# A decoder trunk in float32: the weight ring in pairs, and the 7-product sets at other places

## The chip, the cores and the metric

One core of one Trainium2 chip. The time is device microseconds of one execution; a kernel's time is the median of its runs. In the profile, PE is TensorE's matmul, PEld its weight load, DVE VectorE, ACT ScalarE, POOL GpSimd, SP SyncE, whose queue issues most DMAs.

## The reference

Four layers, sequence 256, width 1024, all float32. Each layer is a half-step SwiGLU feed-forward block (FFN, inner width 2816), a token mixer with memory cross-attention, and a second FFN; the mixers are a gating MLP (layers 0 and 3), dilated window attention (layer 1) and forgetting attention (layer 2).

```
def swiglu_ffn(x, w_gate_up, w_down):
    gate, up = jnp.split(x @ w_gate_up, 2, axis=-1)
    return (jax.nn.silu(gate) * up) @ w_down
...
for i in range(DEPTH):
    kind, j = i % 3, i // 3
    g = norm_g[i]
    x = x + 0.5 * rms_norm(swiglu_ffn(rms_norm(x, g[0]), ffn_w_gate_up[i, 0], ffn_w_down[i, 0]), g[1])
    h = rms_norm(x, g[2])
    ...  # y = mixer a, b or c of h and the normalized memory
    x = x + rms_norm(y, g[3])
    x = x + 0.5 * rms_norm(swiglu_ffn(rms_norm(x, g[4]), ffn_w_gate_up[i, 1], ffn_w_down[i, 1]), g[5])
```

## The kernel before

**Products in three parts.** Every float32 operand is split into a rounded part `hi` and a rest `lo` (`split`: ACT copies to `hi`, DVE subtracts to get `lo`), and a product is hi·hi + hi·lo + lo·hi, accumulated in PSUM.

**The weight ring.** The host packs all weights in the order of use into units of 128 x 1024. `plan()` lists the units: g and u (a quarter of the rows of a gate or up set of 512 columns), e (the same for a set of half width, gate and up in one), D (one block of 128 rows of the down weight), R, C, K, V and O in the mixers, and S (below). `load_next` fetches a unit into one of 5 `raw` tiles over SP's queue; `split_next` makes `hi` and `lo` of it in a ring of 10 tiles each, and asks for the next raw unit. `take` hands a unit to PE's code; `slot(free)`, called once for each unit that PE has read, counts the units released, issues one quadrant load if one is due, takes one background step (`bg`), and calls `pump`, which splits up to two more units as long as the ring has room: about 8 units ahead of PE.

**The FFN** (`ffn`). The 22 blocks of 128 inner columns are cut into six sets (`WIDTH`, four blocks each, one set with two). The first set runs in two halves of the rows and holds its 8 g/u units for both. Two of the others run plainly (`half`), the one of half width too, and three as *7-product sets* (`SEVEN`, `seven`): a 2x2 block product in seven products instead of eight (Strassen-Winograd). For these the four weight quadrants b11, b12, b21, b22 (`quad`, 1 MB each) are loaded whole, in 8 loads in the order b11, b21, b12, b22; a DMA from POOL's queue adds b22 to b12 (`gather`, L271); operation 2 adds b12 to b11 on DVE (L285) and b11 to b21 by another such DMA; operation 4 subtracts b22 from b11 (L288). The seven operands are split into two S units each (`S` with operation and half), and PE multiplies them with sums of the input's quadrants (`left`), 6 products of 512 columns a unit, where other units have 12. Between operations, copies (`snap`, L632) and sums (L644, L655, L661, L666, L667) move between PSUM and SBUF: an operation that adds on to a bank must wait for the copy or the reading of that bank.

The products with the down weight (D units, `fill`) are put between the sets by the table `FILL`; the last 8 run at the end, over the first half of the rows and then over the second, while the norm's steps (`ln_stages`: ACT's squares, DVE's L378, L382, L389, two small operations on POOL at L351 and L352) and the transposes of the result (L403, split into `xth`/`xtl`) run beside them. `new_quad` begins the loads of a set's quadrants: for the first 7-product set ahead of the first set, for the others at the start of the set ahead of them. The tiles of the quadrants are shared with the mixers' `mgh`, `mgl` and with the norm's `rows`, so a load also waits for their last readers.

**Order.** The code is written in program order; a scheduler in the tile layer may move instructions of an engine where their operands come later, and each tile's next user waits for its last reader.

Of the kernel before, what the change touches and what calls it, by code (L numbers as in the profile page):

```python
# [10 lines left out]
F32 = mybir.dt.float32  # L11
# [7 lines left out]
P = 128  # L19
# [11 lines left out]
LN_EPS = 1e-5  # L31
BIG = 1e30
RING = 10
RAW = 5
HELD = 8
GRP = 4

# [168 lines left out]
class Trunk:  # L206
    def __init__(self, ctx, tc, io):
        self.ctx, self.tc, self.nc, self.io = ctx, tc, tc.nc, io
        pool = lambda name, bufs=1, **kw: ctx.enter_context(tc.tile_pool(name=name, bufs=bufs, **kw))
        self.const = pool("const")  # L210
        self.wp = pool("wp")
        self.main = pool("main")
        self.small = pool("small", 4)
        self.ps = pool("ps", space=bass.MemoryType.PSUM)
        self.dram = pool("dram", space=bass.MemoryType.DRAM)
        self.plan = plan()
        self.offs = {}
# [5 lines left out]
        self.raw_order = [key for key in self.plan if key[0] != "S"]  # L223
        self.loaded = self.split_n = self.taken = self.released = 0
# [5 lines left out]
        self.quad_loads = deque()  # L230

    def rot(self, *shape):
        t = self.ps.tile([P, 512], F32, tag="rot", name="rot", bufs=4)
# [10 lines left out]
    def load_next(self):  # L244
        if self.loaded == len(self.raw_order):
            return
        key = self.raw_order[self.loaded]
        a, b = unit_shape(key)
        t = self.wp.tile([P, 1024], F32, tag="raw", name="raw", bufs=RAW)
        self.fetch(t[:, :a * b], key)  # L250
        self.raws.append((t, a * b))
        self.loaded += 1

    def new_quad(self, fp, l, f, s):
        self.quad = [None] * 4
        self.quad_pool = fp
        self.quad_set = (l, f, s)
        self.quad_loads = deque(quads(l, f, s))

# [13 lines left out]
    def quads_for(self, key):  # L273
        if self.quad is None or self.quad_set != key[1:4]:
            return None
        return max(0, len(self.quad_loads) - (QUADS - ((2 * key[4] if key[4] < 2 else 6) + key[5] + 1)))
# [5 lines left out]
    def operand(self, op, h):  # L282
        b11, b12, b21, b22 = (t if t is None else t[:, h, :] for t in self.quad)
        if op == 2:
            self.nc.vector.tensor_tensor(out=b11, in0=b11, in1=b12, op=ALU.add)  # L285
            self.gather(b21, b11)
        elif op == 4:
            self.nc.vector.tensor_tensor(out=b11, in0=b11, in1=b22, op=ALU.subtract)  # L288
        return (b11, b21, b11, b12, b11, b21, b22)[op]

    def split_next(self):
        key = self.plan[self.split_n]
        hi = self.wp.tile([P, 1024], F32R, tag="hi", name="hi", bufs=RING)
        lo = self.wp.tile([P, 1024], F32R, tag="lo", name="lo", bufs=RING)
        if key[0] == "S":
            for _ in range(self.quads_for(key)):
                self.load_quad()
            self.split(hi, lo, self.operand(*key[4:]))
        else:
            t, n = self.raws.popleft()  # L300
            self.split(hi[:, :n], lo[:, :n], t[:, :n])
            self.load_next()
        self.ready.append((hi, lo))
        self.split_n += 1

    def pump(self, lag=1, most=2):
# [230 lines left out]
    def ffn(self, l, f, post_next, pre_next, last=False):  # L537
        nc, tc = self.nc, self.tc
        with tc.tile_pool(name=f"ffn{l}{f}", bufs=1, reuse_waits="tile") as fp:
# [15 lines left out]

            def turn_set(s, t):
                if t == 0:
                    if WIDTH[s] == 2:
                        hs[s] = tuple(fp.tile([P, 2, SEQ], F32R, tag=n, name=n) for n in ("eh", "el"))
                    else:  # L560
                        hs[s] = tuple(fp.tile([P, 4, SEQ], F32R, tag=n, name=n, bufs=2) for n in ("hh", "hl"))
                n = WIDTH[s]
                ps = self.rot()
                for k in range(n):
                    nc.tensor.transpose(ps[:, k * P:(k + 1) * P], T[s][t][:, k * P:(k + 1) * P], self.ident)  # L565
                self.split(*(h[:, :n, t * P:(t + 1) * P] for h in hs[s]),
                           ps[:, :n * P].rearrange("p (k t) -> p k t", k=n))
# [3 lines left out]
            def first_set():  # L571
                T[0] = [tile_T(), tile_T()]
                held = [self.take("g", l, f, 0, i) for i in range(4)]
                for t in range(2):
                    g = self.rot()
                    for i in range(4):
                        pair(held[i], g, i, t)
                        self.slot(t)
                    silu(T[0][t], g)
                    u = self.rot()  # L580
                    if t == 0:
                        held.extend(self.take("u", l, f, 0, i) for i in range(4))
# [5 lines left out]
                    nc.vector.tensor_tensor(out=T[0][t], in0=T[0][t], in1=u, op=ALU.mult)  # L588
# [189 lines left out]

    def mem_kv(self, l):
        nc = self.nc  # L780
        km = self.mp.tile([P, 2, SEQ], F32, name="km")
        vm = self.mp.tile([P, 2, SEQ], F32, name="vm")
# [58 lines left out]
        return got[0]  # L841

    def q_mem(self, l, c0, xt):
        qm = self.mp.tile([P, 2, SEQ], F32, name="qm")
# [503 lines left out]
```

## Time and profile before

| | before |
|---|---|
| median of 3 runs | 1889.15 us (1886.43 to 1889.77) |
| the profiled execution | 1888.2 us, span 1886.4 us |
| mean granted clock | 0.996 |
| HBM read | 359.95 MB |

The span is the time from the first to the last instruction of the profiled execution; the execution's own time has 1.8 us more around it. A group's line gives the busy time, the mean of one in ns, and the idle time ahead of it with what ended it. A row of waits gives the total in us, how many, and the longest. A matmul's busy time includes its passage through the array, in which the next one may already run.

### The profile page before, as it was taken

The page shows a single profiled execution, that of the slowest core. Times are in us where ns is not written, and L with a number is a line of the kernel's source. Part 1 is how long each engine was busy: PE and PEld are TensorE (multiplying, and loading weights), DVE is VectorE, ACT ScalarE, POOL GpSimd, SP SyncE. Part 2 cuts the span into 40 slices and gives each one's busy share as a digit, 9 for nine tenths or more (in the row PEclk, how much of TensorE's full clock was granted, in tenths as well). Part 3 has the DMA queues.
Part 4 walks back from the last instruction along what each step waited for, and adds up shares of the span by engine and source line. Part 5 has one row for each costly group of instructions (what it writes and reads, how often), then busy time and mean ns, then how long its engine had stood idle before and what let it go on. Part 6 is the DMA issues. An engine that isn't in the chain of part 4 may idle for free.

```text
span 1886.4 us, 25346 instructions
## 1 busy us (share of the span) xinstructions
PE 1842.0 (98%) x9310; PEld 1535.2 (81%) x9310; DVE 1537.1 (81%) x1868; ACT 1132.7 (60%) x1541; POOL 150.2 (8%) x211
## 2 busy tenths in 40 slices
PE   7999999999999999999999999999999999999998
PEld 5788887878788797778878889877788888987886
DVE  6888878987988768888789876879887988879884
ACT  5666656656665655656666666556665666656652
POOL 0000201000100100100010000010001000201000
PEclk9999999999999999999999999999999999999999
DMA  8886748776786662677668667358775786738862
GB/s 295 257 265 225 224 136 264 227 243 223 226 261 194 235 220 101 201 242 247 215 210 263 211 218 257 105 190 256 247 245 169 245 264 204 247 125 273 256 192 78
DMA packets 117692, 413.01 MB, mean 219 GB/s; under 512 B 13620, under 2 KB 18112, under 8 KB 117440
## 3 DMA queue, kind: packets, MB, share of 16 engines
q1 hardware_dynamic: 103568, 359.47, 54.2%
q0 software_dynamic: 14000, 51.92, 13.8%
q8 instruction: 73, 1.20, 0.3%
q14 instruction: 51, 0.42, 0.1%
HBM read 359.95 MB, written 1.06 MB: 191 GB/s over the span
## 4 chain that ended last, share of the span: by engine, by line
PE 41%; DVE 7%; DMA 3%; issue 2%; ACT 1%; POOL 1%; DVEq 0%; ACTq 0%; POOLq 0%
PE acc L696 12%; PE rot L624 9%; PE rot L337 5%; PE rot L339 5%; PE rot L338 5%; DVE lo L313 5%; PE acc L960 2%; DMA quad<-quad 2%; DMA quad<-in_w 1%; PE rot L565 1%; PE acc L880 1%; DVE quad L288 1%; PE rot L894 1%; PE rot L862 1%; ACT hi L312 0%
## 5 line engine op out<-in xcount | busy, mean ns | idle before, releaser
L313 DVE TENSOR_TENSOR lo<-raw,hi 128x1024 fp32r<-128x1024 f32 (+2 forms) x451 | 536.3, 1217 | 77.6 <-ACT hi L312 74.7
L312 ACT ACTIVATE hi<-raw 128x1024 fp32r<-128x1024 f32 (+2 forms) x451 | 463.2, 1051 | 198.3 <-DMA raw<-in_w 96.7
L312 ACT ACTIVATE hi<-quad 128x1024 fp32r<-128x1024 f32 x336 | 343.6, 1053 | 227.5 <-DVE quad L285 131.8
L313 DVE TENSOR_TENSOR lo<-quad,hi 128x1024 fp32r<-128x1024 f32 x336 | 397.5, 1219 | 20.7 <-ACT hi L312 19.9
L339 PE MATMUL rot<-hi,xtl 128*128 128x512 f32 (+3 forms) x816 | 312.8, 384 | 3.9 <-DVE xtl L313 3.9
L337 PE MATMUL rot<-hi,xth 128*128 128x512 f32 (+3 forms) x816 | 315.0, 386 | 0.4 <-ACT hi L312 0.4
L338 PE MATMUL rot<-lo,xth 128*128 128x512 f32 (+3 forms) x816 | 312.0, 382 | 0.3 <-DVE lo L313 0.3
L624 PE MATMUL rot<-hi,sums 128*128 128x512 f32 x768 | 255.1, 398 | 16.2 <-ACT snap L632 8.0
L696 PE MATMUL acc<-hi,hh 128*128 128x512 f32 x640 | 199.4, 391 | 0.0
L696 PE MATMUL acc<-lo,hh 128*128 128x512 f32 x640 | 198.9, 390 | 0.0
L696 PE MATMUL acc<-hi,hl 128*128 128x512 f32 x640 | 197.9, 390 | 0.0
L624 PEld LDWEIGHTS rot<-hi,sums 128*128 128x128 f32 x768 | 145.8, 190 | 52.9 <-ACT snap L632 12.3
L339 PEld LDWEIGHTS rot<-hi,xtl 128*128 128x128 f32 x816 | 153.7, 188 | 37.0 <-DVE xtl L313 8.3
L337 PEld LDWEIGHTS rot<-hi,xth 128*128 128x128 f32 x816 | 153.8, 189 | 29.2 <-ACT hi L312 1.0
L338 PEld LDWEIGHTS rot<-lo,xth 128*128 128x128 f32 x816 | 153.8, 188 | 29.2 <-DVE lo L313 0.5
L624 PE MATMUL rot<-lo,sums 128*128 128x512 f32 x384 | 151.2, 394 | 2.1 <-DVE lo L313 2.1
L271 POOL DMA_DIRECT2D quad<-quad x96 | 83.7, 897 | 837.6 <-DMA quad<-in_w 394.5
L696 PEld LDWEIGHTS acc<-hi,hl 128*128 128x128 f32 x640 | 119.6, 188 | 26.9 <-DVE hl L313 2.2
L696 PEld LDWEIGHTS acc<-lo,hh 128*128 128x128 f32 x640 | 119.9, 188 | 24.7
L696 PEld LDWEIGHTS acc<-hi,hh 128*128 128x128 f32 x640 | 119.7, 188 | 24.5
L624 PE MATMUL rot<-hi,xtl 128*128 128x512 f32 x288 | 112.1, 389 | 0.0
L624 PE MATMUL rot<-hi,xth 128*128 128x512 f32 x288 | 112.0, 389 | 0.0
(214 smaller groups left out, 2571.3 us busy)
## 6 DMA issues: line engine op xcount, KB each, us to landing
raw<-in_w SPq DMA_DIRECT2D x440, 512.0 KB, 4.8
quad<-in_w SPq DMA_DIRECT2D x192, 512.0 KB, 5.1
quad<-quad POOLq DMA_DIRECT2D x96, 512.0 KB, 4.7
gpre<-in_norm_g SPq DMA_DIRECT2D x8, 512.0 KB, 6.3
gpost<-in_norm_g SPq DMA_DIRECT2D x8, 512.0 KB, 3.4
memraw<-in_mem_t SPq DMA_DIRECT2D x32, 128.0 KB, 3.6
g<-in_norm_g SPq DMA_DIRECT2D x8, 512.0 KB, 6.7
raw<-in_w SPq DMA_DIRECT2D x8, 384.0 KB, 4.1
```

Source lines behind the costliest of these rows:

```text
L271: self.nc.gpsimd.dma_start(out=x, in_=y, accum_op=ALU.add)
L288: self.nc.vector.tensor_tensor(out=b11, in0=b11, in1=b22, op=ALU.subtract)
L312: self.nc.scalar.activation(out=hi, in_=src, func=AF.Copy)
L313: self.nc.vector.tensor_tensor(out=lo, in0=src, in1=hi.bitcast(F32), op=ALU.subtract)
L337: mm(out, a[0], b[0], start=start, stop=False)
L338: mm(out, a[0], b[1], start=False, stop=False)
L339: mm(out, a[1], b[0], start=False, stop=stop)
L565: nc.tensor.transpose(ps[:, k * P:(k + 1) * P], T[s][t][:, k * P:(k + 1) * P], self.ident)
L624: nc.tensor.matmul(ps, a[i], w[j][:, kk, :], start=fresh and h == kk == i == j == 0, stop=h == kk == i == 1, skip_group_check=True)
L696: mm(ys[t][:, n * 512:(n + 1) * 512], x, y[:, 0, n * 512:(n + 1) * 512], start=(j == 0 and x is a[0] and y is w[0]), stop=(j == NF - 1 and ...
L862: nc.tensor.transpose(ps[:, i * P:(i + 1) * P], blocks[b0 + i], self.ident)
L960: self.nc.tensor.matmul(o["y"][t][:, h * 512:(h + 1) * 512], x, y[:, 0, h * 512:(h + 1) * 512], start=(j == 0 and x is a[0] and y is w[0]) ...
```

## The change

The raw, hi and lo tiles become 2048 columns wide: three raw tiles and five of hi and lo. `groups` pairs neighbouring units of one kind and layer (of one set, for S); a pair is fetched by two DMAs into one raw tile and split by one ACT and one DVE instruction, and a pair's tile comes free when both its units are read. An unpaired unit, or one smaller than 1024, is split by itself. Operation 2's addition and operation 4's subtraction also cover 2048 columns, and so does the DMA that adds b11 to b21.

The half-width set moves from third to second place, so the 7-product sets stand at places 3, 5 and 6 in place of 2, 4 and 6; `FILL` is set anew. The loads of a 7-product set's quadrants begin when the last operation of the one ahead has been split, the first one's in the first set's first half. Of the mixers' tiles, km, vm and qm move into the `snap` tiles, and the half-width set uses hh/hl in place of eh/el.

```
-RAW = 5
+RAW = 3
-WIDTH = (4, 4, 2, 4, 4, 4)
+WIDTH = (4, 2, 4, 4, 4, 4)
+SEVEN = (2, 4, 5)
-SEVEN = (1, 3, 5)
-FILL = {1: (2, 2), 2: (2,), 3: (2, 0), 4: (1, 1), 5: (2, 2)}
+FILL = {1: (2,), 2: (2, 0), 3: (2, 0), 4: (2, 4), 5: (2, 0)}
...
+def groups(order):
+    out = []
+    for key in order:
+        last = out[-1] if out else []
+        if len(last) == 1 and last[0][:2] == key[:2] and (key[0] != "S" or last[0][:5] == key[:5]):
+            last.append(key)
+        else:
+            out.append([key])
+    return out
...
     def load_next(self):
...
+        t = self.wp.tile([P, 2048], F32, tag="raw", name="raw", bufs=RAW)
+        for i, key in enumerate(self.raw_order[self.loaded]):
+            a, b = unit_shape(key)
+            self.fetch(t[:, 1024 * i:1024 * i + a * b], key)
...
-    def new_quad(self, fp, l, f, s):
+    def new_quad(self):
+        self.quad = None
+        if not self.quad_wait:
+            return
+        self.quad_pool, l, f, s = self.quad_wait.popleft()
         self.quad = [None] * 4
...
     def split_next(self):
-        key = self.plan[self.split_n]
-        hi = self.wp.tile([P, 1024], F32R, tag="hi", name="hi", bufs=RING)
+        g = self.groups[self.split_n]
+        hi = self.wp.tile([P, 2048], F32R, tag="hi", name="hi", bufs=RING // 2)
...
+        if g[0][0] == "S":
+            for _ in range(self.quads_for(g[1])):
                 self.load_quad()
-            self.split(hi, lo, self.operand(*key[4:]))
+            self.split(hi, lo, self.operand(g[0][4]))
+            if g[0][4] == 6:
+                self.new_quad()
...
     def pump(self, lag=1, most=2):
-        while most and self.split_n < len(self.plan) and self.split_n < self.released + RING - lag and self.can_split():
+        while most and self.split_n < len(self.groups) and self.units < self.released + RING - lag and self.can_split():
...
             def first_set():
...
                     u = self.rot()
                     if t == 0:
+                        self.quad_wait.extend((fp, l, f, s) for s in SEVEN)
+                        self.new_quad()
...
-            self.new_quad(fp, l, f, 1)
...
-                if s + 1 in SEVEN:
-                    self.new_quad(fp, l, f, s + 1)
...
-        km = self.mp.tile([P, 2, SEQ], F32, name="km")
+        km = self.main.tile([P, 2, SEQ], F32, tag="snap", name="km", bufs=4)
```

SP's queue in the second FFN of layer 0, quadrant loads among the raw loads. Before:

```order
L242 DMA raw<-in_w 128x1024 x8
L242 DMA quad<-in_w 128x1024 x8
L512 DMA rt<-in_inv_freq 128x32
L242 DMA raw<-in_w 128x1024 x2
L242 DMA quad<-in_w 128x1024 x7
L242 DMA raw<-in_w 128x1024 x8
L242 DMA quad<-in_w 128x1024
```

The same place after:

```order
L255 DMA raw<-in_w 128x1024 x10
L255 DMA quad<-in_w 128x1024 x8
L255 DMA raw<-in_w 128x1024 x4
L539 DMA rt<-in_inv_freq 128x32
L255 DMA raw<-in_w 128x1024 x2
L255 DMA quad<-in_w 128x1024 x8
L255 DMA raw<-in_w 128x1024 x12
L255 DMA quad<-in_w 128x1024 x8
```

The second set's eight loads stand six raw units behind the first's, twelve more raw units follow, and the third set's eight come in one piece behind those.

DVE in the last 7-product set of the first FFN of layer 1, from operation 1's sum (L644; L670 in the changed file) to the reading of the bank of operation 4 (L655; L681). Before:

```order
L313 TENSOR_TENSOR lo<-quad,hi 128x1024 x5
L644 TENSOR_TENSOR snap<-snap,rot 128x512
L313 TENSOR_TENSOR hl<-rot,hh 128x4x128 x2
L546 SCALAR_TENSOR_TENSOR T<-T,snap 128x512
L313 TENSOR_TENSOR lo<-quad,hi 128x1024 x3
L313 TENSOR_TENSOR lo<-raw,hi 128x1024 x5
L655 TENSOR_TENSOR snap<-rot,snap 128x512
```

After:

```order
L340 TENSOR_TENSOR lo<-quad,hi 128x2048 x2
L670 TENSOR_TENSOR snap<-snap,rot 128x512
L340 TENSOR_TENSOR lo<-quad,hi 128x2048
L573 SCALAR_TENSOR_TENSOR T<-T,snap 128x512
L340 TENSOR_TENSOR hl<-rot,hh 128x4x128 x2
L340 TENSOR_TENSOR lo<-quad,hi 128x2048
L340 TENSOR_TENSOR lo<-raw,hi 128x2048 x2
L681 TENSOR_TENSOR snap<-rot,snap 128x512
```

The same operations stand there in half as many splits; directly ahead of L681 are two of 2048 columns.

PE in layer 1, where the V units (`rot_5265`, stationary `hi_5243`) follow the transposes of the second half of the rows. After the change:

```order
L366 MATMUL rot_5194<-mgh_4897,lo_5101 128x256
L430 MATMUL rot_5251<-ident_74,rows_5001 128x128 x4
L430 MATMUL rot_5258<-ident_74,rows_5001 128x128 x4
L364 MATMUL rot_5265<-hi_5243,mgh_4897 128x256
L1109 MATMUL rot_5329<-ident_74,ra_5155 128x128 x4
L1118 MATMUL rot_5336<-ident_74,ra_5186 128x128 x4
L1157 MATMUL acc_5579<-qk_5128 128x128
L1157 MATMUL acc_5591<-qk_5128 128x128
L365 MATMUL rot_5265<-lo_5244,mgh_4897 128x256
```

Before, the 48 products with V stood in one piece behind the transposes; now eight transposes and two products stand between the first, which reads `hi`, and the second, which reads `lo`.

More of the change, by code (lines that the diff above doesn't have):

```diff
@@ L222, in __init__ @@
             o += P * a * b
-        self.raw_order = [key for key in self.plan if key[0] != "S"]
-        self.loaded = self.split_n = self.taken = self.released = 0
+        self.groups = groups(self.plan)
+        self.raw_order = [g for g in self.groups if g[0][0] != "S"]
+        self.units = self.loaded = self.split_n = self.taken = self.released = 0
         self.raws = deque()
@@ L230, in __init__ @@
         self.quad_loads = deque()
+        self.quad_wait = deque()
     def rot(self, *shape):
@@ L246, in load_next @@
             return
[L247 to L251, printed above, removed]
-        self.loaded += 1
-    def new_quad(self, fp, l, f, s):
+        t = self.wp.tile([P, 2048], F32, tag="raw", name="raw", bufs=RAW)
+        for i, key in enumerate(self.raw_order[self.loaded]):
+            a, b = unit_shape(key)
+            self.fetch(t[:, 1024 * i:1024 * i + a * b], key)
+        self.raws.append(t)
+        self.loaded += 1
+    def new_quad(self):
[3 more added lines that the diff above has]
+        self.quad_pool, l, f, s = self.quad_wait.popleft()
         self.quad = [None] * 4
-        self.quad_pool = fp
         self.quad_set = (l, f, s)
@@ L275, in quads_for, with operand @@
             return None
-        return max(0, len(self.quad_loads) - (QUADS - ((2 * key[4] if key[4] < 2 else 6) + key[5] + 1)))
+        return max(0, len(self.quad_loads) - (QUADS - (2 * key[4] + key[5] + 1 if key[4] < 2 else 8)))
     def can_split(self):
-        key = self.plan[self.split_n]
+        key = self.groups[self.split_n][-1]
         return key[0] != "S" or self.quads_for(key) == 0
[L282 to L285, printed above, removed]
+    def operand(self, op):
+        add = lambda x, y, f: self.nc.vector.tensor_tensor(out=x, in0=x, in1=y, op=f)
+        b11, b12, b21, b22 = self.quad
+        if op == 4:
+            add(b11, b22, ALU.subtract)
+        elif op == 2:
+            add(b11, b12, ALU.add)
@@ L286, in operand @@
             self.gather(b21, b11)
-        elif op == 4:
-            self.nc.vector.tensor_tensor(out=b11, in0=b11, in1=b22, op=ALU.subtract)
-        return (b11, b21, b11, b12, b11, b21, b22)[op]
+        return (b11, b21, b11, b12, b11, b21, b22)[op].rearrange("p a b -> p (a b)")
     def split_next(self):
-        key = self.plan[self.split_n]
-        hi = self.wp.tile([P, 1024], F32R, tag="hi", name="hi", bufs=RING)
-        lo = self.wp.tile([P, 1024], F32R, tag="lo", name="lo", bufs=RING)
@@ L295, in split_next @@
-        if key[0] == "S":
-            for _ in range(self.quads_for(key)):
+        g = self.groups[self.split_n]
+        hi = self.wp.tile([P, 2048], F32R, tag="hi", name="hi", bufs=RING // 2)
+        lo = self.wp.tile([P, 2048], F32R, tag="lo", name="lo", bufs=RING // 2)
+        if g[0][0] == "S":
+            for _ in range(self.quads_for(g[1])):
                 self.load_quad()
-            self.split(hi, lo, self.operand(*key[4:]))
-        else:
-            t, n = self.raws.popleft()
-            self.split(hi[:, :n], lo[:, :n], t[:, :n])
+            self.split(hi, lo, self.operand(g[0][4]))
+            if g[0][4] == 6:
+                self.new_quad()
+        else:
+            t = self.raws.popleft()
+            n = [a * b for a, b in map(unit_shape, g)]
+            if n == [1024, 1024]:
+                self.split(hi, lo, t)
+            else:
+                for i, w in enumerate(n):
+                    h = slice(1024 * i, 1024 * i + w)
+                    self.split(hi[:, h], lo[:, h], t[:, h])
@@ L302, in split_next @@
             self.load_next()
-        self.ready.append((hi, lo))
+        for i in range(len(g)):
+            self.ready.append((hi[:, 1024 * i:1024 * i + 1024], lo[:, 1024 * i:1024 * i + 1024]))
         self.split_n += 1
+        self.units += len(g)
     def pump(self, lag=1, most=2):
-        while most and self.split_n < len(self.plan) and self.split_n < self.released + RING - lag and self.can_split():
+        while most and self.split_n < len(self.groups) and self.units < self.released + RING - lag and self.can_split():
@@ L557, in turn_set @@
                 if t == 0:
[L558 to L561, printed above, removed]
+                    hs[s] = tuple(fp.tile([P, 4, SEQ], F32R, tag=n, name=n, bufs=2) for n in ("hh", "hl"))
                 n = WIDTH[s]
@@ L780, in mem_kv @@
         nc = self.nc
-        km = self.mp.tile([P, 2, SEQ], F32, name="km")
-        vm = self.mp.tile([P, 2, SEQ], F32, name="vm")
+        km = self.main.tile([P, 2, SEQ], F32, tag="snap", name="km", bufs=4)
+        vm = self.main.tile([P, 2, SEQ], F32, tag="snap", name="vm", bufs=4)
         ps = self.rot().rearrange("p (a b) -> p a b", a=2)
@@ L843, in q_mem @@
     def q_mem(self, l, c0, xt):
-        qm = self.mp.tile([P, 2, SEQ], F32, name="qm")
+        qm = self.main.tile([P, 2, SEQ], F32, tag="snap", name="qm", bufs=4)
         ps = self.in_cols(l, c0, xt)
```

## The prediction

> **What bounds the kernel now.** I read the page's busy times first, then what TensorE waited for, then the stretches in which it waited.
>
> ```profile
> span 1886.4 us, 25346 instructions
> PE 1842.0 (98%) x9310; PEld 1535.2 (81%) x9310; DVE 1537.1 (81%) x1868; ACT 1132.7 (60%) x1541; POOL 150.2 (8%) x211
> 906.95 10.88 PE rot L624 x48
> ```
>
> PE is nearly always busy, and where it waits for nothing, 48 products of 512 columns take 10.88 us, 0.2267 us each. So an S unit (6 products) is consumed in 1.36 us, a D, g, u or e unit (12) in 2.72. The change neither adds nor removes a product. It can win only what PE waits for: 1886.4 - 1842.0 = 44.4 us, itemized here (whole program):
>
> ```profile
> engine line waited for: us in total, times, longest us
> PE rot L403 <- DVE rows L389: 11.6, 6, 8.3
> PE rot L624 <- ACT snap L632: 8.0, 10, 1.6
> PE rot L624 <- DVE snap L655: 4.7, 5, 2.6
> PE rot L339 <- DVE xtl L313: 3.9, 6, 1.2
> PE rot L624 <- ACT hi L312: 3.4, 1, 3.4
> PE rot L624 <- DVE lo L313: 2.1, 1, 2.1
> PE rot L565 <- DVE T L588: 1.5, 1, 1.5
> ```
>
> Of L403's 11.6 us, 8.3 are the start; the other 3.3 and L339's 3.9 lie at the changes of stage (transposes of the normalized rows). These rows make 35.2; smaller ones and the end behind the last product are the other 9.2. The rest stands inside 7-product sets: 8.0 + 4.7 + 3.4 + 2.1 + 1.5 = 19.7 us in 18 waits. A product counts 0.39 us busy though the next may begin 0.227 behind it, so each wait costs 0.16 us more than shown: 18 x 0.16 = 3, together 22.6 us. By place, from the same view in one stretch after another: the second 7-product sets hold 7.0 (seven rows in five sets, their first and last below), the third ones none, so the first ones 12.7; 5.5 of it in layer 0 (the last two rows, PE's own).
>
> ```profile
> PE rot L624 <- DVE snap L655: 2.6, 1, 2.6
> PE rot L624 <- DVE snap L655: 0.5, 1, 0.5
> 46.23 0.51 PE L624 MATMUL rot<-hi,sums 128*128 128x512 f32 x1 [3.40 <-ACT hi L312]
> 48.80 0.79 PE L624 MATMUL rot<-lo,sums 128*128 128x512 f32 x1 [2.06 <-DVE lo L313]
> ```
>
> A second set, PE's wait first, then the chain, DVE and ACT ahead of it:
>
> ```profile
> 843.98 0.50 PE L624 MATMUL rot<-hi,sums 128*128 128x512 f32 x1 [1.27 <-ACT snap L632]
> 829.87 6.43 DMA quad<-quad
> 836.33 1.23 DVE L285 TENSOR_TENSOR quad<-quad 128x1024 f32<-128x1024 f32 x1 [0.83 <-DMA quad<-quad]
> 837.65 1.06 ACT L312 ACTIVATE hi<-quad 128x1024 fp32r<-128x1024 f32 x1 [5.84 <-DVE quad L285]
> 843.35 0.57 ACT L632 ACTIVATE snap<-rot 128x512 f32<-128x512 f32 x1
> ```
>
> The quadrants come late: the DMA that adds one quadrant to another ends at 836.30, DVE's addition (operation 2) waits for it, ACT stands in order behind that for 5.84 us, and the copy (snap) that PE needs before it may go on in the same bank comes out late. A set without this wait costs PE nothing. So the time at stake is in when quadrants arrive, not in DVE's 81%.
>
> **The change, part by part.** *Loads earlier.* Before, the quadrants of a first set were needed directly behind the first set's 8 g/u units. Now four e units (10.9 us) and two D units (5.4 us) stand between: 16.3 us more. The second 7-product set now follows a full set, as the third did before, and that one shows no wait in eight of eight. I count all 22.6 us as won, less 1.5 that may stay in layer 0, where ten raw units now go out ahead of the first quadrant and the loads are late anyway: -21.
>
> *The third 7-product set directly behind the second.* Its loads begin behind the last split of the set ahead, which runs 8 units early. From there PE still has D D, six S units in operations 3 to 5, two in operation 6, and four D: 6 x 2.72 + 8 x 1.36 = 27.2 us to operation 0, 38 to operation 2.
>
> ```profile
> quad<-in_w SPq DMA_DIRECT2D x192, 512.0 KB, 5.1
> quad<-quad POOLq DMA_DIRECT2D x96, 512.0 KB, 4.7
> ```
>
> Eight loads, freed one after another by the splits, are in after some 20 us (4.2 MB at the 219 GB/s mean of the page's DMA row is 19), two accumulating DMAs end 6 later: 26 against 38, hidden. If that cover goes, the set behaves as the second sets do today (7.0 us); the floor is 0. I take 1.5.
>
> ```profile
> DMA packets 117692, 413.01 MB, mean 219 GB/s; under 512 B 13620, under 2 KB 18112, under 8 KB 117440
> ```
>
> *Splits of 2048 columns.* Prices by size, both engines:
>
> ```profile
> L313 DVE TENSOR_TENSOR lo<-quad,hi 128x1024 fp32r<-128x1024 f32 x336 | 397.5, 1219 | 20.7 <-ACT hi L312 19.9
> L313 DVE TENSOR_TENSOR sums<-xf,sums 128x512 fp32r<-128x512 f32 x32 | 21.8, 685 | 0.1
> L312 ACT ACTIVATE hi<-quad 128x1024 fp32r<-128x1024 f32 x336 | 343.6, 1053 | 227.5 <-DVE quad L285 131.8
> L312 ACT ACTIVATE sums<-xf 128x512 fp32r<-128x512 f32 x32 | 19.2, 620 | 9.9 <-DVE xf L607 9.8
> ```
>
> DVE pays 534 ns for 512 more columns, so 2048 cost 1219 + 1068 = 2287 ns, 151 less than two of 1024; ACT 1053 + 866 = 1919, 187 less. The 388 pairs and 48 merged additions save DVE 66 us and ACT 73. All of it lies beside PE: 0 on the path. What reaches PE is the latency: a pair is ready 1.92 + 2.29 = 4.2 us behind its release, where one unit took 1.05 + 1.22 = 2.3. With 8 units ahead (10.9 us at the least) this is hidden, with three exceptions.
>
> (a) Operation 6 adds to a bank that DVE (L655) must read first, with only operation 5 (2.72 us) as cover. Before:
>
> ```profile
> 911.29 2.36 DVE L313 TENSOR_TENSOR lo<-raw,hi 128x1024 fp32r<-128x1024 f32 x2 [0.57 <-ACT hi L312]
> 913.56 0.69 DVE L655 TENSOR_TENSOR snap<-rot,snap 128x512 f32<-128x512 f32 x1
> ```
>
> Now the lo ahead of it is a pair's: released at the end of operation 3 and with 0.2 us for the signal (an estimate), hi ends at 2.1, lo at 4.4, L655 at 5.1, and PE wants it at 2 x 2.72 = 5.44. That leaves 0.3 us, which signals between the engines may use up. Ends: 0, and one L655 (0.68) in each of 24 sets, 16 us. I take 0.1 each: +2.5.
>
> (b) K and V in layers 1 and 2. The ring has five pairs; the held row units take four, K the fifth, and V must wait until both K units are read. Before, the second V unit did so alone:
>
> ```profile
> 671.60 1.06 ACT L312 ACTIVATE hi<-raw 128x1024 fp32r<-128x1024 f32 x1 [1.82 <-PE rot L338]
> 672.26 0.36 PE L337 MATMUL rot<-hi,mgh 128*128 128x256 f32 x1
> 672.69 1.23 DVE L313 TENSOR_TENSOR lo<-raw,hi 128x1024 fp32r<-128x1024 f32 x1 [0.33 <-ACT hi L312]
> ```
>
> Now hi runs 671.60 to 673.52 and lo to 675.8, and PE, which came to V at 672.26, waits up to 3.6 us. In layer 1 eight transposes and two products move into the gap (about 1 us): 2.6 + 3.6 = +6. Ends 0 and 7.2. The layers with a gating mixer hold one pair less and do not wait.
>
> (c) The start. ACT, DVE and PE before:
>
> ```profile
> 8.10 1.06 ACT L312 ACTIVATE hi<-raw 128x1024 fp32r<-128x1024 f32 x1 [2.16 <-DMA raw<-in_w]
> 10.57 1.06 ACT L312 ACTIVATE hi<-raw 128x1024 fp32r<-128x1024 f32 x1 [0.53 <-DMA raw<-in_w]
> 10.33 0.68 DVE L313 TENSOR_TENSOR xtl<-rot,xth 128x512 fp32r<-128x512 f32 x1
> 17.10 0.50 PE L337 MATMUL rot<-hi,xth 128*128 128x512 f32 x1 [0.45 <-ACT hi L312]
> 18.56 0.50 PE L338 MATMUL rot<-lo,xth 128*128 128x512 f32 x1 [0.30 <-DVE lo L313]
> ```
>
> Two transfers (the second half of x, the second unit) take 10.57 - 8.10 = 2.47, so a pair is in at 9.3; hi ends at 11.3, lo at 13.6, and the first xtl, now behind it, at 14.3 instead of 11.0: 3.3 us later. PE waited 0.45 and 0.30 at 17.10 and 18.56 before, with the hidden 0.16 each about 1 us that is swallowed: +2.3, ends 0 and 4.5 (nothing swallowed, and one lo of 1.22 more).
>
> *km, vm, qm in the snap ring, eh/el in hh/hl.* Four buffers as before; the users are read out before their turn comes again in program order. 0.
>
> *Changes of stage.* Rows, x and rows on DVE can stand behind one lo of 2.29 instead of one of 1.22; the same work in half the pieces. Ends -3.6 (half of today's 7.2 of waits goes) and +6.4 (1.07 longer, 2287 - 1219, at as many changes as L403 waits at today, six); I take 0.
>
> A rule speaks against this term. Each turn of the rows has two small POOL operations:
>
> ```profile
> L351 POOL TENSOR_TENSOR r<-ss,thin x48: 186/192/2348, 6.1 to 1879.8; 128x1 f32<-128x1 f32 x48
> L351 POOL TENSOR_TENSOR r<-ss,thin 128x1 f32<-128x1 f32 x48 | 21.5, 449 | 777.4 <-ACT junk L377 681.9 <-ACT junk L385 95.5
> ```
>
> Minimum 186, median 192, longest 2348 ns, mean 449: 48 x 0.257 = 12.3 us are spent blocked, where a lo runs beside. The Trainium skill (SBUF — State Buffer, "Who interferes with whom") says that a VectorE instruction with two SBUF inputs holds a read interface against GpSimd for the whole instruction. These rows agree with it.
>
> **Sum.** -21 + 1.5 + 2.5 + 6 + 2.3 + 0 = -8.7, rounded to -8. The profiled execution took 1888.2 us (its span 1886.4 plus 1.8), 0.95 below the median 1889.15. From the median: 1881.
>
> **Rivals.**
> 1. *All latencies are hidden*: only the gain stays, -21 to -23 and lo work out of the way at stage changes: 1867. For it: PE has 8 units of lead nearly everywhere. Against: (b) has no lead at all.
> 2. *L655 late in every 7-product set* (slower). If a raw transfer is late, or another lo gets ahead, L655 waits behind one more pair. With 1.2 us in each of 24 sets: +29 instead of +2.5, 1881 + 26 = 1907; it turns the sign from about 0.45 us a set. For it: ACT waited 96.7 us for raw units in all. Against: raw units are asked for six ahead.
>
> ```profile
> ACT hi L312 <- DMA raw<-in_w: 96.7, 96, 3.7
> ```
>
> 3. *Blocked POOL operations hand it back.* A lo 2287/1219 = 1.88 times as long blocks 1.88 times as long: 12.3 x 0.88 = 10.8 us more, half of it in the second turns that PE waits for: +5.4, 1886 to 1887, no difference. That is the rule above carried through. Against: in several places the changed order has no lo between the two rows operations.
> 4. *The change doesn't do what it says*: the third set waits as the second ones did (+7.1) and layer 0 keeps its 5.5: 1881 + 5.6 + 4 = about 1890.
>
> **Chances.** My forecast, 1873 to 1885.3: 0.48. Rival 1: 0.17. Rival 2: 0.15. Rivals 3 and 4, within 0.2%: 0.17, and 0.03 that 4 goes further. 0.2% (3.8 us) is about what a measurement can tell from no change. Faster 0.65, same 0.17, slower 0.18. The range reaches from rival 1's end to a mild rival 2 (0.5 us a set): 1866 to 1894.
>
> **What would show it.** Right: no ACT wait on the quadrant additions that reaches PE, the rows of L624 behind hi and lo at 46 us gone, mean lo near 2290 ns, DVE near 1471 us, PE waiting 2 to 4 us at V in layers 1 and 2. Wrong: PE waits behind L655 in many sets, a wait in front of operation 0 or 2 of the last set, longer L403 waits, or a start that loses over 5 us.

## The result: slower, and the profile after

The changed kernel takes 1974.0 us, the median of four runs (1966.6 to 1979.8), against 1889.0 before (four runs, one more than above): a ratio of 1.045, 95% interval 1.0405 to 1.0496. The forecast was 1881. The profiled execution took 1966.6 us and is the fastest of the four.

The page of the changed kernel, with the span and the first row of busy times:

```profile
span 1964.8 us, 23973 instructions
PE 1869.4 (95%) x9310; PEld 1547.2 (79%) x9310; DVE 1505.7 (77%) x1432; ACT 1085.6 (55%) x1153; POOL 127.0 (6%) x187
```

The span grew by 78.4 us. PE's idle time grew from 44.4 to 1964.8 - 1869.4 = 95.4 us, that is +51.0, and its busy time by 27.4 with the same 9310 products. What PE waited for, in total, times and the longest (us):

```profile
PE rot L589 <- DVE T L693: 33.4, 14, 4.4
PE rot L430 <- DVE rows L416: 17.8, 11, 8.1
PE rot L366 <- DVE xtl L340: 7.7, 9, 2.5
PE acc L721 <- DVE hl L340: 4.5, 4, 1.5
PE rot L650 <- DVE snap L681: 3.8, 5, 1.4
PE rot L589 <- DVE T L765: 3.7, 1, 3.7
PE rot L364 <- ACT hi L339: 3.7, 2, 2.6
PE acc L721 <- ACT hh L339: 3.5, 4, 1.2
...
PE rot L650 <- ACT snap L658: 0.4, 1, 0.4
```

The waits of the products inside the 7-product sets (L624, now L650) fell from 18.2 to 4.2 us, as forecast; the prediction's 19.7 has 1.5 of a wait for T with them. In their place stands a new row: 33.4 us in which the transposes (L589) wait for T. L693 is the second of the two DVE operations behind operation 6 (L692 and L693, before L666 and L667); before, no row shows PE waiting for L667.

One such wait in layer 1: DVE, then ACT, then PE, each in its own timeline.

```profile
553.45 0.69 DVE L687 TENSOR_TENSOR T<-T,snap 128x512 f32<-128x512 f32 x1
558.38 2.29 DVE L340 TENSOR_TENSOR lo<-raw,hi 128x2048 fp32r<-128x2048 f32 x1 [4.24 <-ACT hi L339]
560.59 0.68 DVE L692 TENSOR_TENSOR snap<-rot,snap 128x512 f32<-128x512 f32 x1
562.45 2.29 DVE L340 TENSOR_TENSOR lo<-raw,hi 128x2048 fp32r<-128x2048 f32 x1 [1.18 <-ACT hi L339]
564.66 0.69 DVE L693 TENSOR_TENSOR T<-T,snap 128x512 f32<-128x512 f32 x1
```
```profile
556.43 1.92 ACT L339 ACTIVATE hi<-raw 128x2048 fp32r<-128x2048 f32 x1 [5.10 <-DMA raw<-in_w]
560.50 1.91 ACT L339 ACTIVATE hi<-raw 128x2048 fp32r<-128x2048 f32 x1 [2.16 <-DMA raw<-in_w]
```
```profile
565.40 1.97 PE L589 MATMUL rot<-ident,T 128*128 128x128 f32 x8 [3.78 <-DVE T L693]
```

L692 and L693 need no weights. They stand in DVE's order behind two lo's of 2048 columns; each lo waits for a hi, and each hi for a pair of raw units that has not landed. PE, which has units split ahead, waits 3.78 us for T all the same. Over the whole program lo's waits for hi came to 210.0 us, where they were 94.6, before and after:

```profile
DVE lo L313 <- ACT hi L312: 94.6, 108, 3.2
DVE lo L340 <- ACT hi L339: 210.0, 138, 8.8
```

hi's own waits for raw units are no larger in sum, 95.3 us against 96.7, but there are 38 of them in place of 96, so each is longer.

The 27.4 us of busy time come mostly from the clock. The mean granted clock fell from 0.996 to 0.987: in full-clock time, 0.004 x 1886.4 = 7.5 us lost before and 0.013 x 1964.8 = 25.5 now, 18 us more. Stretches of PE (time, busy, granted clock, DMA share, GB/s); the first two follow the 3.78 us wait above, the next two a wait of 2.56 us that ended at 964.30:

```profile
564.00:567.50 3.50, 2.10 (x9) 2.10 (x10) 3.50 (x4) 0.91 (x3) 0.00 (x0) 0.58 0.69 233
567.50:572.00 4.50, 4.50 (x13) 3.46 (x12) 4.04 (x5) 1.10 (x2) 0.00 (x0) 0.57 0.27 109
```
```profile
964.30 0.87 PE L589 MATMUL rot<-ident,T 128*128 128x128 f32 x3 [2.56 <-DVE T L693]
```
```profile
964.30:967.30 3.00, 3.00 (x11) 0.50 0.91 339
967.30:970.30 3.00, 3.00 (x14) 1.00 0.04 14
```

(In the first fence the five pairs of numbers are PE, PEld, DVE, ACT and POOL, then the clock.) Leaving out the start, PE has 13 waits of over 2 us. Behind ten of them the trace shows a stretch at half clock, 3.41 us long or twice that, so such a wait cost PE its length and another 1.7 or 3.4 us. Behind the other three (2.51, 2.89 and 3.02 us) the clock stayed at 1.00.

### The profile page after: what moved, and what is told of

Read it like the earlier page. It is cut to its first block, busy times and chain, and to the rows that moved or that the text cites. A ratio compares the mean times of both kernels' runs of the same rounds, so it can differ in the third digit from the quotient of the medians.

```text
span 1964.8 us, 23973 instructions
## 1 busy us (share of the span) xinstructions
PE 1869.4 (95%) x9310; PEld 1547.2 (79%) x9310; DVE 1505.7 (77%) x1432; ACT 1085.6 (55%) x1153; POOL 127.0 (6%) x187
## 4 chain that ended last, share of the span: by engine, by line
PE 58%; DMA 17%; DVE 13%; issue 7%; ACT 3%; POOL 1%; SPq 1%; DVEq 0%; ACTq 0%; POOLq 0%
PE acc L721 14%; PE rot L650 12%; DVE lo L340 8%; PE rot L366 8%; PE rot L364 8%; PE rot L365 8%; DMA raw<-in_w 7%; DMA quad<-quad 6%; ACT hi L339 3%; PE acc L983 3%; DMA quad<-in_w 2%; PE rot L589 2%; DVE quad L299 1%; PE rot L885 1%; PE acc L903 1%
## 5 line engine op out<-in xcount | busy, mean ns | idle before, releaser
L340 DVE TENSOR_TENSOR lo<-raw,hi 128x2048 fp32r<-128x2048 f32 (+2 forms) x231 | 511.7, 2223 | 148.9 <-ACT hi L339 145.7
L339 ACT ACTIVATE hi<-raw 128x2048 fp32r<-128x2048 f32 (+2 forms) x231 | 429.2, 1861 | 246.5 <-DMA raw<-in_w 95.3
L339 ACT ACTIVATE hi<-quad 128x2048 fp32r<-128x2048 f32 x168 | 320.5, 1914 | 255.4 <-DVE quad L299 157.0
L340 DVE TENSOR_TENSOR lo<-quad,hi 128x2048 fp32r<-128x2048 f32 x168 | 382.3, 2285 | 64.3 <-ACT hi L339 64.3
L650 PE MATMUL rot<-hi,sums 128*128 128x512 f32 x768 | 253.3, 396 | 4.2 <-DVE snap L681 3.8
L721 PE MATMUL acc<-hi,hh 128*128 128x512 f32 x704 | 221.8, 393 | 3.6 <-ACT hh L339 3.5
L721 PE MATMUL acc<-hi,hl 128*128 128x512 f32 x704 | 219.8, 392 | 4.5 <-DVE hl L340 4.5
L721 PE MATMUL acc<-lo,hh 128*128 128x512 f32 x704 | 218.8, 392 | 0.0
L650 PEld LDWEIGHTS rot<-hi,sums 128*128 128x128 f32 x768 | 145.0, 189 | 39.7 <-DVE snap L681 9.2
L299 DVE TENSOR_TENSOR quad<-quad 128x2048 f32<-128x2048 f32 x48 | 109.9, 2290 | 68.6 <-DMA quad<-quad 45.5
L721 PEld LDWEIGHTS acc<-hi,hl 128*128 128x128 f32 x704 | 132.5, 189 | 33.6 <-DVE hl L340 6.3
L650 PE MATMUL rot<-lo,sums 128*128 128x512 f32 x384 | 150.5, 392 | 0.0
L287 POOL DMA_DIRECT2D quad<-quad x72 | 62.7, 882 | 951.9 <-DMA quad<-in_w 435.1
L650 PE MATMUL rot<-hi,xtl 128*128 128x512 f32 x288 | 112.1, 389 | 0.0
```

Source lines behind the costliest of these rows:

```text
L287: self.nc.gpsimd.dma_start(out=x, in_=y, accum_op=ALU.add)
L299: add = lambda x, y, f: self.nc.vector.tensor_tensor(out=x, in0=x, in1=y, op=f)
L339: self.nc.scalar.activation(out=hi, in_=src, func=AF.Copy)
L340: self.nc.vector.tensor_tensor(out=lo, in0=src, in1=hi.bitcast(F32), op=ALU.subtract)
L650: nc.tensor.matmul(ps, a[i], w[j][:, kk, :], start=fresh and h == kk == i == j == 0, stop=h == kk == i == 1, skip_group_check=True)
L721: mm(ys[t][:, n * 512:(n + 1) * 512], x, y[:, 0, n * 512:(n + 1) * 512], start=(j == 0 and x is a[0] and y is w[0]), stop=(j == NF - 1 and ...
```

## The experiments

Line numbers shift by a few between these kernels: T's last operation is L692, L693, L694, L696 or L703, the copy `snap` L656 to L661. Each time is a median with its ratio to the kernel before, timed on the same chip.

### Undoing parts of the change

**e1_late_quads.** The wait above follows eight quadrant loads in SP's queue. Here the second 7-product set's loads begin later.

```
-                self.new_quad()
+                if g[0][3] == SEVEN[0]:
+                    self.quad = None
+                else:
+                    self.new_quad()
...
+                    if s - 1 == SEVEN[0]:
+                        self.new_quad()
```

> Pairs and the new order stay; only the quadrant loads of the 7-product set at place 5 begin later: not behind the last split of the set at place 3, but when PE turns that set's result (three units into the full set between them). Theory A (the early loads stand in SP's queue ahead of raw units that are needed sooner, a late raw unit holds DVE in order, and T at L693 behind it comes late to PE): the waits of L589 at the six places behind the first 7-product set (2.3 to 4.4 us each, 20 to 24 us with their slow-clock stretches 30 to 35) go, the others stay: 1935 to 1948. Theory B (what costs is the length of a split of 2048 columns on DVE, wherever raw comes from): 1965 to 1980, as the changed kernel (1974). Theory C (the order of the sets itself leaves too little between op 6 and the transposes): also 1965 to 1980.

1967.7 us, 1.0429 (1.0386 to 1.0471). The waits for T stayed (27.9 us in 12, and 3.80 where 3.78 is shown above). The early quadrant loads are not what makes them.

**e2_half_ops.** Tiles, loads and releases in pairs, but each pair split by two ACT and two DVE instructions of 1024.

```
-            self.split(hi, lo, self.operand(g[0][4]))
+            src = self.operand(g[0][4])
+            for i in range(2):
+                h = slice(1024 * i, 1024 * i + 1024)
+                self.split(hi[:, h], lo[:, h], src[:, h])
```

> Everything as in the changed kernel, tiles and loads in pairs too, but each pair is split by two ACT and two DVE instructions of 1024 columns. Theory A: the raw units come just as late; 1960 to 1978. Theory B (length of the instructions): DVE can slip L692, L693, the rows and hl between halves, most of the 47 us of added waits go: 1900 to 1925, though DVE is busy for 60 us more. Theory C: 1965 to 1980.

1928.4 us, 1.0216 (1.0184 to 1.0249): 46 us come back, close to theory B, whose range ended at 1925. Waits for T:

```profile
PE rot L592 <- DVE T L696: 10.8, 9, 3.1
```

**e3_order_only.** The new order, FILL, load times and shared tiles with single units.

```
-RAW = 3
+RAW = 5
...
-        if len(last) == 1 and ...:
+        if False and len(last) == 1 and ...:
...
-        hi = self.wp.tile([P, 2048], F32R, tag="hi", name="hi", bufs=RING // 2)
+        hi = self.wp.tile([P, 1024], F32R, tag="hi", name="hi", bufs=RING)
...
```

> The new order of the sets, the new fills and the loads begun at the last split ahead, but the ring of single units as before (10 tiles of 1024, 5 raw tiles). Theory A with the queue alone: the quadrants still stand ahead of the raw units, so L693 is late as well: 1935 to 1960. Theory B (pairs cost): 1870 to 1890, the forecast gain of some 10 to 20 us without the pairs' price. Theory C: 1940 to 1975.

1883.5 us, 0.9979 (0.9965 to 0.9992). Its waits:

```profile
PE rot L588 <- DVE T L692: 9.9, 7, 3.5
PE acc L720 <- ACT hh L338: 5.0, 3, 2.4
PE rot L649 <- ACT snap L657: 1.9, 2, 1.1
```

The order does win the in-set waits (18.2 to 2.1, with 0.2 for L680), but T (9.9 against 1.5 us) and hh (5.0 against none) are waited for instead, and most of it is given back there. FILL now has zeros behind operation 6 of the first and the last 7-product set, where two D units stood, so T has less cover there; e8 below tests that.

**e4_pairs_old_order.** Pairs, with the order, FILL and load times of before.

```
-WIDTH = (4, 2, 4, 4, 4, 4)
-SEVEN = (2, 4, 5)
+WIDTH = (4, 4, 2, 4, 4, 4)
+SEVEN = (1, 3, 5)
-FILL = {1: (2,), 2: (2, 0), 3: (2, 0), 4: (2, 4), 5: (2, 0)}
+FILL = {1: (2, 2), 2: (2,), 3: (2, 0), 4: (1, 1), 5: (2, 2)}
...
```

> The pairs of the change with the order, the fills and the load times of before (single D units of the one-unit fills are split alone). Theory A: with the loads begun at the start of the set ahead the raw units are not held up as much; 1890 to 1915. Theory B (pairs cost): 1940 to 1980. Theory C (order): 1885 to 1900.

1950.2 us, 1.0325 (1.0298 to 1.0352). In the old order, where two of the three 7-product sets have D units behind operation 6, the waits fall on the copy instead:

```profile
PE rot L648 <- ACT snap L656: 20.9, 17, 3.5
```

So the pairs cost some 61 us in the old order and 90 in the new one. What in them?

### Which part of the pairs

**e5_ring_pairs.** As e2, with raw units single again.

```
-        t = self.wp.tile([P, 2048], F32, tag="raw", name="raw", bufs=RAW)
+        t = self.wp.tile([P, 1024], F32, tag="raw", name="raw", bufs=RAW)
...
+                t = self.raws.popleft()
+                self.split(hi[:, h], lo[:, h], t[:, :a * b])
+                self.load_next()
```

> As the experiment with half the instruction length (1928 us), but the raw units are loaded, held (five tiles of 1024) and asked for one by one; hi/lo tiles, the release and the quadrant additions stay in pairs. Theory of the raw grain (a pair must have landed whole, and its tile is asked for again only when the whole pair is split): most of the 45 us that are left between 1883 and 1928 come back, 1890 to 1900. Rival, the grain of the hi/lo ring (both units of a pair must be read before the next pair may be written, and both are emitted together, so four splits stand ahead of whatever comes next on DVE): no gain, 1922 to 1932. Rival, the merged additions: no gain either, and the next kernel shows it.

1965.7 us, 1.0418 (1.0382 to 1.0455): 37 us worse than with raw units in pairs, and above the ranges of the theory and of its rivals. The theory of the raw grain fell.

**e6_merged_adds.** As e3, with only the additions and their DMA merged; as in the changed kernel, all eight quadrant loads are then due when operation 2 is split.

```
-        if op == 2:
-            self.nc.vector.tensor_tensor(out=b11, in0=b11, in1=b12, op=ALU.add)
+        if (op, h) == (4, 0):
+            add(b11, b22, ALU.subtract)
+        elif (op, h) == (2, 0):
+            add(b11, b12, ALU.add)
             self.gather(b21, b11)
...
```

> As the kernel with single units and the new order (1883 us), but operation 2's addition and operation 4's subtraction cover 2048 columns, the DMA that adds b11 to b21 moves 1 MB, and all eight quadrant loads are due at operation 2. If the merged additions carry the rest of the pairs' price: 1900 to 1925. If not: 1880 to 1890, within 0.4% of 1883.

1966.2 us, 1.041 (1.0368 to 1.0452): +83 us, beyond what I had allowed. PE's idle time grew by 56.1 us against e3 (42.1 to 98.2), and one row is two thirds of that:

```profile
PE rot L650 <- ACT snap L658: 40.6, 9, 5.9
```

In layer 0's second FFN, DVE, ACT and PE:

```profile
432.22 2.29 DVE L299 TENSOR_TENSOR quad<-quad 128x2048 f32<-128x2048 f32 x1 [6.90 <-DMA quad<-quad]
442.38 2.29 DVE L299 TENSOR_TENSOR quad<-quad 128x2048 f32<-128x2048 f32 x1 [0.89 <-DVE lo L340]
```
```profile
434.63 2.01 ACT L339 ACTIVATE hi<-quad 128x1024 fp32r<-128x1024 f32 x2 [12.47 <-DVE quad L299]
444.79 1.06 ACT L339 ACTIVATE hi<-quad 128x1024 fp32r<-128x1024 f32 x1 [4.36 <-DVE quad L299]
445.75 0.58 ACT L658 ACTIVATE snap<-rot 128x512 f32<-128x512 f32 x1
```
```profile
446.39 0.80 PE L650 MATMUL rot<-hi,sums 128*128 128x512 f32 x1 [5.89 <-ACT snap L658]
```

At the same place in e3 the first half was added while the second was on its way:

```profile
413.49 1.22 DVE L301 TENSOR_TENSOR quad<-quad 128x1024 f32<-128x1024 f32 x1 [1.19 <-DMA quad<-quad]
417.13 1.23 DVE L301 TENSOR_TENSOR quad<-quad 128x1024 f32<-128x1024 f32 x1 [1.81 <-DMA quad<-quad]
```

The merged operation 2 cannot begin on its first half while the second half's transfer is on its way; ACT stands 12.47 us behind it, the splits shift, and operation 4's hi, waiting for its own merged subtraction, stands ahead of the copy that PE needs.

**e7_raw_pairs.** As e3, with only the raw units in pairs (three tiles of 2048, which hold six units in place of five, asked for again when the second unit is split).

```
-        t = self.wp.tile([P, 1024], F32, tag="raw", name="raw", bufs=RAW)
+        t = self.wp.tile([P, 2048], F32, tag="raw", name="raw", bufs=RAW)
...
-            self.load_next()
+            if end:
+                self.load_next()
...
```

> As the kernel with single units and the new order (1883 us), but raw units are fetched in pairs into three tiles of 2048, and a tile is asked for again when its second unit is split; hi, lo and all instructions stay at 1024. Theory of the raw grain: 1895 to 1925, with longer waits of hi for raw. Rival (the ring's grain or the additions): 1880 to 1890.

1877.2 us, 0.9946 (0.9927 to 0.9965), below both ranges: this part of the change helps, by 6 us. Whether by the pairs or by the room for a sixth unit is not shown.

**e8_fill_tail.** As e3, with cover for T and hh, and six raw tiles.

```
-RAW = 5
+RAW = 6
-FILL = {..., 4: (2, 4), 5: (2, 0)}
+FILL = {..., 4: (2, 2), 5: (2, 2)}
-                    ps = half("e", s, after, 2)
+                    ps = half("e", s, after, 1)
```

> As the kernel with single units and the new order (1883 us), with six raw tiles in place of five, two D units moved from behind the second 7-product set to behind the third (FILL 4: (2, 2), 5: (2, 2)), so that 5.4 us more of products stand between the last operation and the transposes of T, and in the half-width set the first set's turn one unit earlier (2.7 us more ahead of the first D unit). Where waits for T (9.9 us in 7) and for hh/hl (5.0 + 1.1) are what is left: 1868 to 1875. Rival: the third set directly behind the second now has 5.4 us less cover for its quadrants, and waits for them by 1 to 3 us in eight sets: 1883 to 1900.

1889.4 us, 1.0016 (0.9998 to 1.0034). The waits for T and hh went, but the rival came: the third set lost its lead. Eight of the ten waits in this row stand there:

```profile
PE rot L649 <- DVE snap L680: 16.6, 10, 2.5
```

**e9_half_adds.** The changed kernel with additions and their DMA in halves; splits stay at 2048.

```
...
+        for h in range(2):
+            if op == 4:
+                add(b11[:, h, :], b22[:, h, :], ALU.subtract)
+            elif op == 2:
+                add(b11[:, h, :], b12[:, h, :], ALU.add)
+                self.gather(b21[:, h, :], b11[:, h, :])
```

> The changed kernel (1974 us), with only operation 2's addition, operation 4's subtraction and the DMA behind operation 2 cut back into two of 1024 columns (512 KB); raw, hi and lo stay in pairs with splits of 2048. Merging them alone cost 83 us in the kernel with single units. Theory of the merged additions: 1885 to 1915. Rival, length of the splits: 1950 to 1975, no more than the additions' own 1 us each comes back, since the split behind them still needs both halves.

1951.2 us, 1.0332 (1.0303 to 1.036): 23 us come back, as the rival had it.

**e10_half_all.** Both: every instruction at 1024, tiles and loads in pairs.

```
...
+            for i in range(2):
+                h = slice(1024 * i, 1024 * i + 1024)
+                self.split(hi[:, h], lo[:, h], self.operand(g[0][4], i))
...
```

> The changed kernel with every instruction on S and raw units cut into two of 1024 and emitted half by half (addition, hi, lo, then the second half); tiles, loads and releases stay in pairs. The kernel with half splits but merged additions took 1928 us. Theory of the merged additions: 1878 to 1895, near the kernel with raw units in pairs alone (1877). Rival, grain of the hi/lo ring: 1915 to 1930.

1904.7 us, 1.0094 (1.0079 to 1.0109), between the two theories: the hi/lo ring in pairs has a price of its own. It is 27.6 us above e7 (1877.2), from which it differs in the ring (tiles and releases in pairs, two units taken up together) and in the due time of the loads, which cost nothing with single units (f2 below). Part of it is the change of stage, where e7 has 1.7 us of waits for xtl:

```profile
PE rot L368 <- DVE xtl L342: 13.5, 10, 3.2
```

**e11_before_merged.** The kernel before, with e6's edit alone.

> The kernel before, with operation 2's addition, operation 4's subtraction and the DMA behind operation 2 merged to 2048 columns (1 MB) and all eight quadrant loads due at operation 2; nothing else. Theory of the merged additions, whatever the order of the sets: 1920 to 1970 (the old order with everything in pairs took 1950). Rival, the merged additions cost only where the third 7-product set stands directly behind the second: 1889 to 1900.

1936.3 us, 1.0249 (1.0225 to 1.0273). The merged additions cost 49 us in the old order too.

**f2_due_early.** As e3, with e6's due time for the loads but the additions in halves.

```
-QUADS - ((2 * key[4] if key[4] < 2 else 6) + key[5] + 1)
+QUADS - (2 * key[4] + key[5] + 1 if key[4] < 2 else 8)
```

> As the kernel with single units and the new order (1883 us), additions and their DMA in halves, but all eight quadrant loads due when operation 2 is split, as the merged additions need it. If the due time carries the 81 us of the merged additions: 1940 to 1970, with quadrant loads ahead of raw loads in SP's order. If it is the additions themselves: 1880 to 1890.

1883.7 us, 0.9975 (0.9962 to 0.9987), as e3. The due time costs nothing there; it is the additions and their transfer.

**f3_raw_pairs_merged.** As e7, with e6's edit.

> As the kernel with raw units in pairs (1877 us), with the merged additions and all eight loads due at operation 2. If the merged additions cost the same in every ring: 1950 to 1965. If raw units in pairs take most of their price away, as the difference between 1966 and 1928 us of the two kernels with a paired ring suggests: 1900 to 1925.

1913.0 us, 1.0139 (1.0097 to 1.0181): 36 us where it cost 83 with single raw units.

All with the new order, in us:

| raw | hi/lo tile | split | additions | time |
|---|---|---|---|---|
| pair | pair | 2048 | 2048 | 1974.0 (the change) |
| pair | pair | 2048 | 1024 | 1951.2 (e9) |
| pair | pair | 1024 | 2048 | 1928.4 (e2) |
| pair | pair | 1024 | 1024 | 1904.7 (e10) |
| pair | unit | 1024 | 2048 | 1913.0 (f3) |
| pair | unit | 1024 | 1024 | 1877.2 (e7) |
| unit | pair | 1024 | 2048 | 1965.7 (e5) |
| unit | unit | 1024 | 2048 | 1966.2 (e6) |
| unit | unit | 1024 | 1024 | 1883.5 (e3) |

Down from the change by e2 or e9, then e10 and e7: the length of the splits 46 us (45.6 and 46.5), the merged additions 23 (22.8 and 23.6), the hi/lo ring in pairs 28; together 97, from 1974 to 1877. The last two depend on which is undone first: by e2, f3 and e7 the ring is worth 15 (1928.4 to 1913.0, f3's runs being spread from 1907 to 1926) and the additions 36. With single raw units the additions cost 83 and the ring 0 (e5, e6). So only the 97 and the 46 are firm here; the other 51 are what ring and additions cost together.

### The mechanism itself

**f1_hold_splits.** The changed kernel, every instruction as long as before, but no new split is taken up between operation 5 and the two DVE operations behind operation 6.

```
-                    self.slot(1)
+                    self.slot(1, hold=op == 5 or (op == 6 and h == 0))
...
-        self.pump()
+        if not hold:
+            self.pump()
```

> The changed kernel (1974 us), but no new splits are taken up between operation 5 of a 7-product set and the two DVE operations behind operation 6, so that no lo stands ahead of these in program order; the splits follow directly behind. Theory (in-order DVE: T waits behind lo's whose hi waits): the 33.4 us of waits for T and their half-clock stretches mostly go, 1920 to 1945. Rival (data late anyway, or the lead of three units that is given up comes back as waits of the next units): 1960 to 1990.

1934.6 us, 1.0262 (1.0226 to 1.0298): 39 us come back from when the splits are taken up, with their length unchanged. Busy times, then PE's waits for T, then DVE at the place shown above:

```profile
PE 1859.0 (96%) x9310; PEld 1540.0 (80%) x9310; DVE 1500.6 (78%) x1432; ACT 1080.2 (56%) x1153; POOL 128.3 (7%) x187
```
```profile
PE rot L590 <- DVE T L694: 5.1, 2, 4.5
```
```profile
554.29 0.69 DVE L688 TENSOR_TENSOR T<-T,snap 128x512 f32<-128x512 f32 x1
554.90 0.68 DVE L693 TENSOR_TENSOR snap<-rot,snap 128x512 f32<-128x512 f32 x1
559.34 2.29 DVE L340 TENSOR_TENSOR lo<-raw,hi 128x2048 fp32r<-128x2048 f32 x1 [3.75 <-ACT hi L339]
561.55 0.68 DVE L694 TENSOR_TENSOR T<-T,snap 128x512 f32<-128x512 f32 x1
```

The lo still waits 3.75 us for its late hi, but one lo fewer stands ahead of T, which is out at 562.2 in place of 565.3, and PE does not wait there. Waits for T fell from 33.4 to 5.1 us and PE's busy time by 10.4 (1869.4 to 1859.0).

### A version that beats both

**e12_raw_pairs_turn.** As e7, with the first set's turn one unit earlier in the half-width set.

```
-                    ps = half("e", s, after, 2)
+                    ps = half("e", s, after, 1)
```

> As the kernel with the new order, single hi/lo and raw units in pairs (1877 us), with the transposes of the first set one unit earlier in the half-width set (behind its second unit in place of its third). There 6.7 us of waits for hh and 0.7 for hl were left, each in front of the first D unit behind that set. If the 2.7 us of cover hold: 1868 to 1873. Rival, the splits stand in ACT's order just the same: 1875 to 1879.

1871.1 us, 0.9913 (0.9899 to 0.9928).

```profile
span 1867.9 us, 25204 instructions
PE 1837.2 (98%) x9310; PEld 1535.5 (82%) x9310; DVE 1539.8 (82%) x1868; ACT 1146.6 (61%) x1543; POOL 148.8 (8%) x211
```

PE is idle for 30.7 us, 8.2 of them the wait for the first rows at the start. DVE and ACT are busier than in the changed kernel, and the kernel is 103 us faster.

## Why the prediction was wrong

**The step that failed** is the one on splits of 2048 columns: "All of it lies beside PE: 0 on the path", and "With 8 units ahead (10.9 us at the least) this is hidden, with three exceptions". The lead protects only PE's own reading of weights. It does nothing for work that PE needs soon and that stands behind a split in DVE's or ACT's order (f1 shows it: holding the splits back from ahead of T brought 39 us): T behind operation 6, the copies, hh and hl, rows and xtl. I looked for such a place at L655 and, with 0 as the result, at the changes of stage. The price in place of 0 is 97 us: the length of the splits 46, the merged additions and the hi/lo ring together 51. (f1's 39 are no further price: it takes away the same waits as shorter splits do.)

**The saving on DVE and ACT** was oversized too: 66 and 73 us forecast, 31.4 (1537.1 to 1505.7) and 47.1 (1132.7 to 1085.6) measured. One lo of 2048 took 2.287 us, as forecast; but two of 1024 back to back overlap and take 2.36, as a row quoted in the prediction says, not twice 1.219. A pair saves some 0.07 us where its instructions stand together, and the first unit is ready 1.1 us later for it.

**Merged additions**: I counted them with the splits as 48 instructions saved. What they take away is the overlap of the first half's work with the second half's transfer. Alone they cost 49 us in the old order.

**A wait's price**: I added 0.16 us for each. The clock behind the longer ones cost another 18 us in all, against the 7.5 of before.

**Loads earlier, -21**: right in place and about right in size (the waits in the sets 18.2 to 4.2; to 2.1 with single units). But the order, with FILL, gave most of it to T and hh, so that alone it is worth about 4 us (e3). What covers those two I had not asked.

**Third set, +1.5**: right for this FILL in that its quadrants came in time: L650 waits for no copy there. 3.5 of the 3.8 us of waits for L681, counted under (a), do stand in third sets. With e8's FILL, two D units fewer ahead of it, L649's waits came to 18.3 in all (16.6 and 1.7). One step of the working is off: four S units behind 27.2 us make 32.6 to operation 2, not 38, which is still above 26.

**(a) L655, +2.5**: it waits 3.8 in 5 places, not in 24; rival 2 named the right mechanism at the wrong operation. The 0.2 us for a signal came from no row: in the trace of before, the 240 ACT instructions that waited for a product began 0.04 us behind its end in the median. **(b) K and V, +6**: waits of 1.05, 2.61 and 0.62 us appear in layers 1 and 2, 4.3 together, in the places forecast. **(c) The start, +2.3**: 1.9 and 1.0 of new waits in place of 0.45 and 0.30, so +2.2; hi ended at 11.47 and lo at 13.79, where I had 11.3 and 13.6.

**Changes of stage, 0**: L430's waits without the start went from 3.3 to 9.7, xtl's from 3.9 to 7.7: +10.2, above the end of +6.4 that I gave.

**Rival 3**, more time blocked on POOL, did not come. With lo 1.88 times as long, the mean of the first operation rose by 4%, 449 to 465 ns:

```profile
L378 POOL TENSOR_TENSOR r<-ss,thin 128x1 f32<-128x1 f32 x48 | 22.3, 465 | 749.8 <-ACT junk L404 644.3 <-ACT junk L412 105.5
```

The rule in the Trainium skill (SBUF — State Buffer, "Who interferes with whom") on a read interface held for a whole instruction does not by itself size this. The trace has 20 of these 48 operations longer than 300 ns, where there were 15, but most begin late in a lo and wait for its tail only: over the median of 192 ns they lose 13.1 us in all, against 12.4 before.

**Still open**: why merged additions cost 83 us with single raw units and 36 or 23 with pairs; which of the two merged additions and the larger transfer carries it, as no run merges one alone; and how the hi/lo ring's 15 to 28 us divide between the common release, the four splits taken up together and, in this ring, the loads' due time.

## What to carry to other kernels

A larger instruction saves its engine's time and lengthens the wait of everything behind it in that engine's order; when the engine is not the bound, only the second counts. So before merging, list the small operations on the same queue that the bottleneck engine waits for, and what each may stand behind, the producer's own waits included. A merge that joins two halves also gives up the overlap between one half's transfer and the other half's work.

## What the runs showed of the hardware

PE's half-clock stretches, without the start and the end, are 3.41 us long or a small multiple of that in every trace here. They follow waits of under 3 us too: 2.31 us (ending at 376.87) and 2.56 us were followed by 3 us at 0.50, while after 2.51 (ending at 211.18), 2.89 (1852.37) and 3.02 us (1061.33) the clock stayed at 1.00. Over the traces of all runs, half clock began behind all 41 waits of over 3.41 us, behind 67 of 93 between 1.9 and 3.41, and behind 19 of 160 between 0.9 and 1.9.

The Trainium skill (TensorE: Matmul & The Clock Gate, "Part 1: The HAM clock gate") gives about one free-running window of 3.4 us of idling as the condition. The length of the stretches and the waits over 3.41 us agree with that; the shorter waits that were followed by half clock do not, and here the measurement decides. That the length alone does not decide fits a window that runs on its own, which no run here isolated.
